# Gates and the inputs of an SSD scan, projected in one phase by block products and kept in DRAM

## The chip, the cores and the metric

One core of a Trainium2 chip runs the kernel alone. The metric is the device time of one execution in microseconds, as the median of several runs. Of the core's engines, TensorE (PE) multiplies matrices into PSUM, VectorE (DVE), ScalarE (ACT) and GpSimd (POOL) work element by element, and SyncE (SP) issues the DMAs. Each has its own queue of instructions, and semaphores tie them together.

## The reference

One layer of a hybrid encoder trunk on 1024 frames of 1024 features, in float32: a mixer of two parallel branches with a residual, a SwiGLU block with a residual, a last norm.

```python
D_MODEL = SEQ = 1024; CONV_W = 4; SSD_INNER = 2048; SSD_HEADS = 32; SSD_GROUPS = 4; SSD_STATE = 128

def hybrid_mixer(xn, w_in, ...):
    proj = xn @ w_in
    lru_x, lru_gate, z, xbc, dt_raw, gates = _split(proj, IN_WIDTHS)   # 1024, 1024, 2048, 3072, 32, 2048
    u = causal_dw_conv(lru_x, lru_conv_w, lru_conv_b)
    h = rg_lru(u, ...)
    y_a = gelu(lru_gate) * h
    xbc = silu(causal_dw_conv(xbc, ssd_conv_w, ssd_conv_b))
    xs, Bm, Cm = _split(xbc, (2048, 512, 512))
    dt = softplus(dt_raw + ssd_dt_bias)
    y = ssd_scan(xs, dt, -exp(ssd_A_log), Bm, Cm) + ssd_D[:, None] * xs
    y = y * silu(z)
    yg = y.reshape(bsz, s, 4, 512)
    yg = yg * rsqrt(mean(yg * yg, axis=-1) + EPS)
    y_b = yg.reshape(bsz, s, 2048) * ssd_norm_g
    g_a, g_b = _split(sigmoid(gates + b_gate), (1024, 1024))
    merged = g_a * (y_a @ w_branch[:1024]) + g_b * (y_b @ w_branch[1024:])
    return merged @ w_out

h = x + hybrid_mixer(rms_norm(x, norm1_g), ...)
h = h + (silu(n @ w_gate) * (n @ w_up)) @ w_ffn_out          # n = rms_norm(h, norm2_g)
return rms_norm(h, norm_f)
```

## The kernel before

Every matrix is held as two parts, a rounded one and the rest (`split`, on ACT and DVE), and a product is three matmuls: high by high, high by low, low by high. A matmul has 128 rows of weights and 512 columns, so 128 output features on all 1024 frames take 8 blocks of the sum x 2 halves x 3 = 48 matmuls (`mm_ch`). Weights come through a plan (`add`, `w_next`): a raw block is loaded into one of two buffers, split, and used in the order of the plan.

The order of the work is this. Norm 1 makes `xn_hi` and `xn_lo`, transposed, 64 KB per partition, which stay until the last gate. The LRU branch has eight tiles, each with two projections, a convolution read out of PSUM (`conv`) and a tail on ACT and DVE (`lru_tail`), whose result goes to DRAM. Then the SSD scan runs over four groups of eight chunks of 128 frames. A group needs one tile of B, one of C and four of x (`xbc`: 48 matmuls, convolution, Silu), and z of each chunk (`gate_z`: 24 matmuls). `chunk_in` forms the decay matrix of a chunk from a row of cumulated decays read from DRAM (a difference on DVE, a mask on POOL, an exp on ACT), the scores and the transposed x; `chunk_out` multiplies, carries the state on, multiplies with Silu of z, normalizes each row and stores it. Projections of the next group stand by hand between chunks 2 and 5. Two gate tiles stand behind the last chunk. Then the branch product (`wb`), where the normalized rows come back and are transposed (`add_v`); then gates and merges by turns (`gate`, `gate_b`, `merge`); the out projection and norm 2; the first FFN product in seven block products instead of eight (`unit_sums`, `opened`, `after`); the second FFN product.

The Tile framework schedules the instructions: what stands earlier in the program has priority, and within that an instruction goes where a model of the engines sees it ready. Tiles with one tag rotate through `bufs` buffers; a pool opened where another was closed lies on its memory and waits tile by tile for its last readers.

These lines carry the step that the change rewrites in the scan:

```python
nc.vector.tensor_tensor(out=ed, in0=ed, in1=bcast(acs_t[:, c, hs], P), op=ALU.subtract)      # L541
nc.scalar.activation(out=ed, in_=ed, func=AF.Exp)                                            # L545
r = rsqrt_dve(pp, ss, 1.0 / GC)                                                              # L611
nc.vector.scalar_tensor_tensor(out=yf, in0=yf, scalar=r[:, 0:1], in1=g_bc, op0=ALU.mult, op1=ALU.mult)   # L612
```

## Time and profile before

| | |
|---|---|
| time, median of 3 runs | 2077.08 us (2075.48 to 2077.55) |
| the profiled execution, its own time | 2076.53 us |
| its span, first to last instruction | 2074.8 us |
| mean granted TensorE clock | 0.993 |
| PE, DVE, ACT, POOL busy | 2014.5, 1215.4, 837.7, 520.6 us |
| matmuls (and transposes) | 9212 |
| DMA traffic | 182 MB, mean 88 GB/s |

A profile is one execution on the chip. Lines such as L132 are lines of the program, and a line can be a helper's. A matmul's own duration (about 0.39 us) is longer than its place in the queue, since matmuls overlap; so its cost is read from a stretch that is full of them. The granted clock is 1.00 at 2.4 GHz and 0.50 at 1.2 GHz. In the chain of waits each piece is what released the next one.

### The profile page before, as it was taken

How to read it: one execution, taken by the hardware profiler on the slowest of the kernel's cores; microseconds unless marked ns; L12 is line 12 of the kernel's file. 1: busy time of each engine (PE TensorE's matmuls, PEld its weight loads, DVE VectorE, ACT ScalarE, POOL GpSimd, SP SyncE). 2: the span in 40 equal slices, each digit the busy share in tenths (PEclk: the TensorE clock that was granted, in tenths of full speed). 3: DMA queues.
4: the chain of work that ended last, by engine and by line, in shares of the span. 5: the costliest groups of instructions: out<-in, count | busy, mean ns of one | idle time of the engine just before them, and what ended most of it. 6: DMA issues, size and time to landing. Idle time of an engine off the chain costs nothing.

```text
span 2074.8 us, 23723 instructions
## 1 busy us (share of the span) xinstructions
PE 2014.5 (97%) x9212; PEld 1652.6 (80%) x9212; DVE 1215.4 (59%) x1906; ACT 837.7 (40%) x1172; POOL 520.6 (25%) x364
## 2 busy tenths in 40 slices
PE   5999999999999999899999999998999999999998
PEld 4778888878788788688888888886888888888887
DVE  7677676887877877624432123567555555546445
ACT  5877653554544544531131113344323233342112
POOL 3101004525526436300101100036433433303000
PEclk9999999999999999999999999999999999999999
DMA  4221241231322322323232112521232232256212
GB/s 134 62 68 58 61 127 51 88 100 57 92 82 67 110 73 62 101 86 93 63 115 61 51 41 82 191 93 62 72 102 72 71 102 81 76 187 194 82 61 81
DMA packets 178804, 182.27 MB, mean 88 GB/s; under 512 B 9404, under 2 KB 145028, under 8 KB 178692
## 3 DMA queue, kind: packets, MB, share of 16 engines
q1 hardware_dynamic: 178692, 180.76, 28.0%
q8 instruction: 72, 1.18, 0.2%
q14 instruction: 40, 0.33, 0.1%
HBM read 148.10 MB, written 32.64 MB: 87 GB/s over the span
## 4 chain that ended last, share of the span: by engine, by line
PE 78%; DVE 11%; DMA 3%; POOL 2%; issue 2%; ACT 2%; SPq 0%; POOLq 0%; DVEq 0%; ACTq 0%
PE mm L132 35%; PE mm L810 20%; PE mm L143 13%; PE aux L143 6%; DMA ed<-acs_dram 2%; DVE rs_t L155 1%; DVE ed L541 1%; DMA w_raw<-in_w_in_dram 1%; PE aux L421 1%; PE aux L587 1%; DVE rs_r L156 1%; DVE xd L612 1%; DVE wz L81 1%; DVE rs_t L154 1%; PE turn L512 1%
## 5 line engine op out<-in xcount | busy, mean ns | idle before, releaser
L810 PE MATMUL mm<-slot,wc 128*128 128x512 f32 x1848 | 426.9, 392 | 6.3 <-DVE slot L914 5.1
L810 PEld LDWEIGHTS mm<-slot,wc 128*128 128x128 f32 x1848 | 346.9, 188 | 84.7 <-DVE slot L914 6.7
L132 PE MATMUL mm<-xn_hi,w_hi 128*128 128x512 f32 x896 | 354.1, 395 | 1.6 <-DVE xs_a L312 1.1
L132 PE MATMUL mm<-xn_hi,w_lo 128*128 128x512 f32 x896 | 353.3, 395 | 0.0
L132 PE MATMUL mm<-xn_lo,w_hi 128*128 128x512 f32 x896 | 352.2, 393 | 1.1 <-DVE xn_lo L202 1.1
L143 PE MATMUL mm<-slot,slot 128*128 128x512 f32 (+1 forms) x924 | 213.6, 387 | 0.0
L132 PEld LDWEIGHTS mm<-xn_lo,w_hi 128*128 128x128 f32 x896 | 169.2, 189 | 38.7 <-DVE xn_lo L202 1.4
L132 PEld LDWEIGHTS mm<-xn_hi,w_hi 128*128 128x128 f32 x896 | 169.2, 189 | 38.3 <-DVE xs_a L312 1.9
L143 PEld LDWEIGHTS mm<-slot,slot 128*128 128x128 f32 x924 | 171.5, 188 | 34.8
L132 PEld LDWEIGHTS mm<-xn_hi,w_lo 128*128 128x128 f32 x896 | 169.1, 189 | 37.1
L81 DVE TENSOR_TENSOR w_lo<-w_raw,w_hi 128x1024 fp32r<-128x1024 f32 x80 | 108.1, 1351 | 138.4 <-ACT w_hi L80 138.3
L143 PE MATMUL mm<-wz,xn_hi 128*128 128x512 f32 x512 | 164.0, 398 | 0.0
L80 ACT CAST w_hi<-w_raw 128x1024 fp32r<-128x1024 f32 x80 | 83.5, 1043 | 172.9 <-PE mm L132 152.1
L143 PE MATMUL aux<-slot,slot 128*128 128x512 f32 x528 | 124.4, 389 | 0.0
L143 PEld LDWEIGHTS aux<-slot,slot 128*128 128x128 f32 x528 | 99.1, 188 | 20.6
L143 PEld LDWEIGHTS mm<-wz,xn_hi 128*128 128x128 f32 x512 | 96.0, 190 | 18.9
L143 PE MATMUL mm<-wz,xn_lo 128*128 128x512 f32 x256 | 101.8, 398 | 0.0
L848 POOL TENSOR_TENSOR u_u<-u_u,e 128x512 f32<-128x512 f32 x22 | 28.8, 1310 | 248.2 <-DVE u_u L842 238.4
L81 DVE TENSOR_TENSOR wc<-s,wc 128x512 fp32r<-128x512 f32 x88 | 76.4, 908 | 23.0 <-ACT wc L80 23.0
L132 PE MATMUL mm<-v_even,w_hi 128*128 128x512 f32 x256 | 84.7, 405 | 2.2 <-ACT v_even L201 2.2
L132 PE MATMUL mm<-v_odd,w_hi 128*128 128x512 f32 x256 | 81.9, 398 | 0.0
L80 ACT CAST slot<-w_raw 128x1024 fp32r<-128x1024 f32 x34 | 35.5, 1051 | 110.2 <-PE mm L143 50.0
(273 smaller groups left out, 3298.0 us busy)
## 6 DMA issues: line engine op xcount, KB each, us to landing
w_raw<-in_w_in_dram SPq DMA_DIRECT2D x72, 512.0 KB, 3.9
ed<-acs_dram SPq DMA_DIRECT2D x32, 512.0 KB, 3.6
w_raw<-in_w_branch_dram SPq DMA_DIRECT2D x24, 512.0 KB, 3.5
w_raw<-in_w_ffn_in_dram SPq DMA_DIRECT2D x22, 512.0 KB, 4.1
raw_pair<-in_w_ffn_in_dram SPq DMA_DIRECT2D x22, 512.0 KB, 4.3
act_dram<-act SPq DMA_DIRECT2D x22, 512.0 KB, 2.6
act_raw<-act_dram SPq DMA_DIRECT2D x22, 512.0 KB, 3.5
w_raw<-in_w_ffn_out_dram SPq DMA_DIRECT2D x22, 512.0 KB, 4.7
```

The lines of the kernel that those rows point to most:

```text
L80: nc.scalar.copy(out=hi, in_=src)
L81: nc.vector.tensor_tensor(out=lo, in0=src, in1=f32(hi), op=ALU.subtract)
L132: nc.tensor.matmul(ps[:m, :], ww[:, k, :], xx(p, k, h), start=(k == 0 and i == 0), stop=(k == nk - 1 and i == 2))
L143: nc.tensor.matmul(ps, xx(p, k), ww(q, k), start=(k == 0 and i == 0), stop=(k == nk - 1 and i == 2))
L154: nc.vector.tensor_tensor(out=t, in0=r, in1=r, op=ALU.mult)
L155: nc.vector.scalar_tensor_tensor(out=t, in0=t, scalar=-0.5, in1=v, op0=ALU.mult, op1=ALU.mult)
L156: nc.vector.scalar_tensor_tensor(out=r, in0=t, scalar=1.5, in1=r, op0=ALU.add, op1=ALU.mult)
L421: nc.tensor.matmul(pg, w[:, j, :], uu[:, hs], start=(q == 0), stop=(q == 2))
L512: nc.tensor.transpose(out=pt[:, i * P:(i + 1) * P], in_=raw[:, o:o + P], identity=ident)
L541: nc.vector.tensor_tensor(out=ed, in0=ed, in1=bcast(acs_t[:, c, hs], P), op=ALU.subtract)
L810: nc.tensor.matmul(ps, w[:, p, k, :], x[q][:, k, :], start=(start and k == 0 and i == 0), stop=(k == 3 and i == 2), skip_group_check=True)
L848: nc.gpsimd.tensor_tensor(out=d["u3"], in0=d["u3"], in1=d["e5"], op=ALU.add)
```

## The change

Behind norm 1 stands a new phase. The normalized input is kept in four quarter blocks (`xq`: two halves of the features by two halves of the frames, each in two parts). While norm 1 still turns the second half of the frames, the first halves of the gates of branch a are made on the first half of the frames (`g_first`, `g_second`), and the first of the seven products is put into DRAM for later (`e1_dram`). `row_sums` forms four sums of the quarter blocks (t1 to t4). Then 20 units run, twelve for pairs of tiles of x, B and C and eight for pairs of gates (one of branch a, one of branch b): seven products of 12 matmuls each, of which a gate unit makes five here. x, B and C are convolved from SBUF (`conv_rows`), passed through Silu and stored in DRAM; gates go through a sigmoid and into DRAM. LRU follows, both halves of each projection in it. The scan loads B, C and x by tile (`rows_of`) while the group before runs, and projects z alone, for the next group in chunks 6 and 7. In a chunk the difference on DVE becomes the bias of eight exps (one per head) on ACT; the gain of the norm moves to where rows are transposed in the branch product; two chunks share one reciprocal root, and ACT does the final scaling. Buffers for z, for the output rows and for x go up. The merges load gates (`gate_in`) instead of projecting them.

```diff
+    xq = [[[quad(slot(1)) for h in range(2)] for kh in range(2)] for p in range(2)]
...
+    def g_first(m):
+        b = bank("mm")
+        hi, lo = gw[m]
+        product(b, hi[:, 0:4], lo[:, 0:4], xc["b11"], True)
+        e1 = hbuf("e1")
+        nc.scalar.copy(out=e1, in_=b)
+        nc.sync.dma_start(out=e1_dram[m], in_=e1)
+        return b
...
+    def row_sums(k):
+        ks = slice(k, k + 2)
+        f = {}
+        for kh in range(2):
+            for h in range(2):
+                f[kh, h] = ubuf(f"f{kh}{h}", [P, 2, 512])
+                (nc.vector if kh == 0 else nc.gpsimd).tensor_tensor(
+                    out=f[kh, h], in0=f32(xq[0][kh][h][:, ks]), in1=f32(xq[1][kh][h][:, ks]), op=ALU.add)
...
+        nc.vector.tensor_tensor(out=f11, in0=f12, in1=f11, op=ALU.subtract)
+        parts("t1", f11)
+        nc.gpsimd.tensor_tensor(out=f12, in0=f22, in1=f12, op=ALU.subtract)
+        nc.vector.tensor_tensor(out=f22, in0=f22, in1=f11, op=ALU.subtract)
+        parts("t2", f22)
+        nc.gpsimd.tensor_tensor(out=f21, in0=f21, in1=f22, op=ALU.subtract)
+        parts("t3", f12)
+        parts("t4", f21)
+    for m in range(3, KT):
+        gw[m] = g_parts(m)
+        gb_[m] = g_first(m)
+        g_second(m - 1, gb_[m - 1])
+        if m == 4:
+            row_sums(0)
+        elif m == 6:
+            row_sums(2)
...
+    for i in range(4):
+        kinds += [("x", 3 * i), ("x", 3 * i + 1), ("g", 2 * i), ("x", 3 * i + 2), ("g", 2 * i + 1)]
...
+    def conv_rows(x, tile_no):
+        t = ubuf("conv", [P, S])
+        tap = [par1[:, j * 24 + tile_no:j * 24 + tile_no + 1] for j in range(4)]
+        nc.scalar.activation(out=t, in_=x, func=AF.Identity, scale=tap[3], bias=par1[:, 96 + tile_no:97 + tile_no])
+        for j in (2, 1, 0):
+            d = 3 - j
+            nc.vector.scalar_tensor_tensor(out=t[:, d:], in0=x[:, :S - d], scalar=tap[j], in1=t[:, d:],
+                                           op0=ALU.mult, op1=ALU.add)
+        nc.scalar.activation(out=t, in_=t, func=AF.Silu)
+        nc.sync.dma_start(out=xbc_dram[tile_no // 2][(tile_no % 2) * P:(tile_no % 2 + 1) * P, :], in_=t)
...
+    for n, (kind, i) in enumerate(kinds):
+        uleft[n] = 7 if kind == "x" else 5
+        useq += [(n, 6), (n, 5)] + [(n, 2)] * (kind == "x") + [(n, 7), (n, 3)]
+        if n + 1 < NU and kinds[n + 1][0] == "x":
+            useq.append((n + 1, 1))
+        useq.append((n, 4))
...
-        for h in range(2):
-            nc.scalar.activation(out=t[:, half(h)], in_=ps[h], func=func,
-                                 bias=par2[:, LG + b * KT + m:LG + b * KT + m + 1])
...
-            ps = mm_ch(w_next(), xn)
-            o = pool.tile([P, S], F32, name=tag, tag=tag, bufs=bufs)
-            conv(o, ps, par1, lambda j: j * 24 + tile_no, 96 + tile_no)
-            nc.scalar.activation(out=o, in_=o, func=AF.Silu)
-            return o
+        def rows_of(tile_no, tag, bufs, pool=pp):
+            t = pool.tile([P, S], F32, name=tag, tag=tag, bufs=bufs)
+            nc.sync.dma_start(out=t, in_=xbc_dram[tile_no // 2][(tile_no % 2) * P:(tile_no % 2 + 1) * P, :])
+            return t
...
-            nc.vector.tensor_tensor(out=ed, in0=ed, in1=bcast(acs_t[:, c, hs], P), op=ALU.subtract)
...
-            nc.scalar.activation(out=ed, in_=ed, func=AF.Exp)
+            for h in range(HG):
+                nc.scalar.activation(out=ed[:, h, :], in_=ed[:, h, :], func=AF.Exp, bias=nacs_t[:, c, h0 + h:h0 + h + 1])
...
-            xd = pp.tile([P, HG, 64], F32, name="xd", tag="xd", bufs=2)
+            xd = pp.tile([P, HG, 64], F32, name="xd", tag="xd", bufs=4)
...
-            r = rsqrt_dve(pp, ss, 1.0 / GC)
-            nc.vector.scalar_tensor_tensor(out=yf, in0=yf, scalar=r[:, 0:1], in1=g_bc, op0=ALU.mult, op1=ALU.mult)
+            pend.append((c, yf))
+            if n:
+                r = rsqrt_dve(pp, ss2[0], 1.0 / GC, 2)
+                for i, (cc, y) in enumerate(pend):
+                    nc.scalar.activation(out=y, in_=y, func=AF.Copy, scale=r[:, i:i + 1])
+                    nc.sync.dma_start(out=y_dram[g][:, :, cc * P:(cc + 1) * P], in_=y.rearrange("p (a b) -> p a b", b=P))
+                pend.clear()
...
-                state = chunk_out(g, c, c_hl, parts, state, szs.pop(0), g_bc)
+                elif g + 1 < NG:
+                    if c + 2 == NC:
+                        wz_next(4)
+                    szs.append(gate_z(g + 1, c + 2 - NC))
+                state = chunk_out(g, c, c_hl, parts, state, szs.pop(0))
```

## Rows read from the trace of the kernel before

**Rows 1.** The page: each engine's busy us, share of the span, instructions.

```profile
PE 2014.5 (97%) x9212; PEld 1652.6 (80%) x9212; DVE 1215.4 (59%) x1906; ACT 837.7 (40%) x1172; POOL 520.6 (25%) x364
```

**Rows 2.** Table by stage: stretch, its length, then busy us (instructions).

```profile
core 0: us, PE busy (x) PEld busy (x) DVE busy (x) ACT busy (x) POOL busy (x), PEclk, DMA share, GB/s
0.00:46.00 46.00, 24.11 (x119) 19.14 (x120) 34.29 (x69) 24.59 (x48) 18.45 (x15) 1.00 0.47 151
457.00:604.20 147.20, 143.27 (x707) 119.01 (x706) 117.45 (x231) 73.99 (x99) 63.04 (x50) 0.99 0.27 81
751.20:875.60 124.40, 116.38 (x584) 95.42 (x584) 85.62 (x181) 57.35 (x84) 61.53 (x48) 0.95 0.24 75
1057.00:1298.00 241.00, 241.00 (x1056) 198.02 (x1055) 65.26 (x73) 57.76 (x74) 17.08 (x6) 1.00 0.25 73
1398.00:1421.00 23.00, 13.57 (x51) 9.34 (x49) 19.75 (x18) 15.83 (x22) 18.56 (x10) 0.93 0.00 1
1421.00:1825.00 404.00, 404.00 (x1765) 331.36 (x1766) 219.87 (x282) 128.32 (x229) 145.93 (x102) 1.00 0.28 86
```

**Rows 3.** Timeline of PE, last group: start us, us, instruction.

```profile
770.67 1.22 PE L587 MATMUL aux<-xdt,ed 128*128 128x64 f32 x10
...
817.91 0.78 PE L587 MATMUL aux<-xdt,ed 128*128 128x64 f32 x6
```

**Rows 4.** Table by stage, in the last group's chunks with z alone beside them.

```profile
771.70:818.70 47.00, 45.79 (x232) 38.16 (x232) 39.40 (x78) 23.58 (x35) 33.23 (x26) 0.93 0.20 63
805.00:810.00 5.00, 4.78 (x16) 3.61 (x15) 2.67 (x7) 0.15 (x1) 2.31 (x2) 0.50 0.41 125
```

**Rows 5.** Groups by line, whole span, DVE: two of FFN, one of LRU.

```profile
L81 DVE TENSOR_TENSOR wc<-s,wc 128x512 fp32r<-128x512 f32 x88 | 76.4, 908 | 23.0 <-ACT wc L80 23.0
L842 DVE TENSOR_TENSOR u_u<-mm,e_sg 128x512 f32<-128x512 f32 x22 | 15.2, 691 | 36.3 <-PE mm L810 36.3
L429 DVE SCALAR_TENSOR_TENSOR th<-gr,th 128x1024 f32<-128x1024 f32 x8 | 9.8, 1222 | 0.2
```

**Rows 6.** LRU's end: the chain of waits on PE, and DVE's timeline.

```profile
249.41 60.21 PE mm L132 x263
...
257.64 1.23 DVE L433 TENSOR_TENSOR gr<-gl,gr 128x1024 f32<-128x1024 f32 x1
```

**Rows 7.** Groups by line of ACT in the second group of the scan.

```profile
L545 ACT ACTIVATE ed<-ed 128x1024 f32<-128x1024 f32 x8 | 8.5, 1060 | 1.8 <-POOL ed L543 1.8
L465 ACT ACT_TABLE_LOAD x5 | 6.4, 1283 | 19.0 <-DVE keep L315 9.4 <-DVE b_ch L315 4.2 <-DVE xs_b L315 3.1
L80 ACT CAST w_hi<-w_raw 128x1024 fp32r<-128x1024 f32 x6 | 6.2, 1033 | 0.0
L565 ACT CAST xw<-xwf 128x512 fp32r<-128x512 f32 x7 | 4.3, 620 | 17.4 <-POOL xwf L563 17.3
L465 ACT ACTIVATE xs_b<-xs_b 128x1024 f32<-128x1024 f32 x3 | 3.2, 1061 | 3.1 <-DVE xs_b L315 3.0
L307 ACT ACTIVATE xs_b<-mm,par 128x512 f32<-128x512 f32 x4 | 3.1, 774 | 1.5 <-PE mm L132 1.5
```

**Rows 8.** Groups by line of DVE in the same stretch.

```profile
L541 DVE TENSOR_TENSOR ed<-ed,acs_t 128x1024 f32<-128x1024 f32 x8 | 12.9, 1612 | 5.2 <-DMA ed<-acs_dram 5.2
L612 DVE SCALAR_TENSOR_TENSOR xd<-xd,rs_r,g_bc 128x512 f32<-128x512 f32 x8 | 7.7, 966 | 0.3
L312 DVE SCALAR_TENSOR_TENSOR xs_b<-mm,par,xs_b 128x509 f32<-128x509 f32 x5 | 3.7, 743 | 0.1
```

**Rows 9.** The chain of waits in the last group: start us, us, what.

```profile
806.78 2.74 DMA y_dram<-xd
```

**Rows 10.** Timeline of ACT in the last group: start us, us, instruction.

```profile
791.49 0.60 ACT L532 ACTIVATE sz<-mm 128x512 f32<-128x512 f32 x1
792.11 1.28 ACT L545 ACT_TABLE_LOAD   x1
793.40 1.06 ACT L545 ACTIVATE ed<-ed 128x1024 f32<-128x1024 f32 x1
```

More of the change, by code (lines that the diff above doesn't have):

```diff
@@ L274, in params, with u_raw, product @@
             nc.vector.tensor_copy(out=dst[:, :n], in_=pt[:, :n])
+    def u_raw(name, col, stage=None):
+        t = stream.tile([P, KT, P], F32, name="w_raw", tag="w_raw", bufs=2) if stage is None else ubuf(name, [P, KT, P])
+        nc.sync.dma_start(out=t, in_=w_cols(w_in, col))
+        return t
+    xc = {"b11": [xq[p][0][0] for p in range(2)], "b21": [xq[p][1][0] for p in range(2)],
+          "b22": [xq[p][1][1] for p in range(2)]}
+    XOF = {1: "b11", 2: "b21", 3: "b22", 4: "t4", 5: "t1", 6: "t2", 7: "t3"}
+    def product(ps, whi, wlo, x, start):
+        for k in range(4):
+            for i, (w, q) in enumerate(((whi, 0), (whi, 1), (wlo, 0))):
+                nc.tensor.matmul(ps, w[:, k, :], x[q][:, k, :], start=(start and k == 0 and i == 0),
+                                 stop=(k == 3 and i == 2), skip_group_check=True)
     norm1_load(0)
@@ new lines, in g_first, with gate_out @@
+    def g_first(m):
[6 more added lines that the diff above has]
+        return b
+    def gate_out(b, m, h, src, dst=None):
+        o = hbuf("g_out") if dst is None else dst
+        nc.scalar.activation(out=o, in_=src, func=AF.Sigmoid, bias=par2[:, LG + b * KT + m:LG + b * KT + m + 1])
+        nc.sync.dma_start(out=g_dram[b][m][:, half(h)], in_=o)
@@ new lines, in g_second @@
+    def g_second(m, b):
+        hi, lo = gw.pop(m)
+        product(b, hi[:, 4:8], lo[:, 4:8], xc["b21"], False)
+        gate_out(0, m, 0, b)
+    gw = {0: g_parts(0)}
+    gb_ = {0: g_first(0)}
+    params()
+    late_rows = [norm1_rows(c) for c in range(4, 6)]
+    gw[1] = g_parts(1)
+    gb_[1] = g_first(1)
+    g_second(0, gb_[0])
+    for i, c in enumerate(range(4, 6)):
+        norm1_turn(c, late_rows[i])
+    late_rows = [norm1_rows(c) for c in range(6, 8)]
+    gw[2] = g_parts(2)
+    gb_[2] = g_first(2)
@@ new lines, in hybrid_block_kernel, with unit_prepare @@
+    HOME = {1: 1, 2: 1, 6: 6, 7: 6, 4: 6, 5: 5, 3: 5}
+    NU = len(kinds)
+    useq, uleft = [(0, 1)], {}
+    for n, (kind, i) in enumerate(kinds):
[4 more added lines that the diff above has]
+        useq.append((n, 4))
+    def unit_prepare(i):
+        if i >= len(useq):
+            return
+        n, p = useq[i]
+        if n not in sums:
+            unit_sums(n)
+        t = ubuf("wc", [P, 2, 4, P], F32R)
+        split(t[:, 0], t[:, 1], sums[n][p])
+        wready[n, p] = t
+        uleft[n] -= 1
+        if uleft[n] == 0:
+            if n + 2 < NU:
+                unit_load(n + 2)
+            elif n + 2 == NU:
+                load_next()
+                load_next()
@@ new lines, in hybrid_block_kernel @@
+    unit_load(0)
+    unit_load(1)
+    ULEAD = 3
+    for i in range(ULEAD):
+        unit_prepare(i)
+    g_second(KT - 1, gb_[KT - 1])
+    for i, (n, p) in enumerate(useq):
+        unit_prepare(i + ULEAD)
+        if HOME[p] == p:
+            banks[n, p] = bank("mm")
+        w = wready.pop((n, p))
+        product(banks[n, HOME[p]], w[:, 0], w[:, 1], xc[XOF[p]], HOME[p] == p)
+        unit_after(n, p)
+    t_stack.close()
+    u_stack.close()
+    wst_stack = ExitStack()
+    wst = wst_stack.enter_context(phase("wst", "right"))
@@ L650, in v_odd, with add_ya, then @@
             return t
+        ya = []
+        def add_ya(j):
+            def then(raw):
+                t = slot(1)
+                split(t[:, 0, :], t[:, 1, :], raw)
+                ya.append(t)
+            add(ya_dram[j * P:(j + 1) * P, :], then)
         for g in range(NG):
@@ L657, in hybrid_block_kernel @@
                     add_v(g + 1, m // 2, v_even if g % 2 else v_odd)
-        add(w_cols(w_in, OFF_G))
+                if g >= 2:
+                    add_ya((g - 2) * 4 + m // 2)
+        for m in range(KT):
+            add(w_cols(w_branch, m * P))
         for g in range(NG):
@@ L741, in hybrid_block_kernel @@
         add_wo(0, 0, wo0)
-        merge(KT - 2, gas.popleft())
-        merge(KT - 1, gas.popleft())
+        gas = deque(gate_in(0, m) for m in range(2))
+        for m in range(KT):
+            gate_b(m)
+            if m + 2 < KT:
+                gas.append(gate_in(0, m + 2))
+            merge(m, gas.popleft())
         w_drain()
@@ L760, in hybrid_block_kernel @@
     split_half(0, 0)
-    r8[1] = ctx.enter_context(phase("r8b"))
     wo1, wo2 = [], []
```

283 lines of the change are left out of this document (149 added, 134 removed).

## The prediction

> **What bounds the kernel now.** I read the page's busy shares first: TensorE (PE) is busy for 2014.5 of 2074.8 us [rows 1], so what it lacks is 60.3 us in all, and any gain must come from PE work or from those 60. The table by stage then shows where they lie [rows 2]: 21.9 us in norm 1, 3.9 to 4.1 us in each of the first three groups of the scan (one row stands for three), 8.0 us in the last group, 9.4 us at the turn from out projection to FFN. The FFN stage, which already uses the seven-product scheme that the change brings to the projections, has PE busy for all of its 404 us, and so has the stretch of gates and merges: 1056 matmuls in 241.0 us, 0.228 us each. That last number is the price of a matmul in all that follows. So the kernel is PE-bound nearly everywhere, the scan included, and the scan is so because projections of B, C and x fill PE between its chunks. Third, the one stretch where chunks run with z alone beside them, in the last group: 771.7 to 818.7 us. Four chunks pass in it (score-times-x products end at 771.9 and at 818.7 us, [rows 3]), 11.7 us per chunk, and there VectorE (DVE) is busy for 39.4 of 47 us, 84%; the granted clock is 0.93 over it, and after PE has small gaps it is 0.50, its lower level, for 5 us [rows 4]. That stretch is what the change makes of the whole scan, with a lighter DVE.
>
> **The change, part by part.** The sum is made against the profiled execution: span 2074.8 us, 2076.5 us with what lies around it, 0.6 us below the median of 2077.1.
>
> *Matmuls.* Before, 24 tiles of B, C, x and 16 of gates take 48 matmuls each: 1920. After, 12 units of B, C, x take 7 products of 12 matmuls, 1008, and 8 units of gates the same 7 products (two of them early, in norm 1), 672: 1680. 240 fewer at 0.228 us is **-54.8 us** on PE [rows 2]. z, LRU, branch and output products keep their counts. This term has one answer wherever PE is the bound.
>
> *Start.* Norm 1 keeps its chain; instead of the first halves of an LRU tile, PE gets 192 matmuls of gate column products on the first half of the rows, 43.8 us, and the LRU halves come later in full. I cost it at 0: the gap up to 46 us is set by x loads and DVE, both unchanged (bounds -3 and +4 us).
>
> *The operand sums.* The blocks t1 to t4 of the normalized input have to be formed and split. DVE has 12 passes of 1024 elements at about 1.2 us for that, some 15 us without and 20 us with a slow GpSimd (POOL) beside it, and PE has five gate columns, 27 us, as cover; DVE also splits five weights in it (7 us) and comes out of norm 1 with 34.3 of 46 us busy [rows 2]. The nearest row is the same step before FFN, 9.4 us of idle PE with a granted clock of 0.93, and that has less cover [rows 2]. I take **+5** (0 to +9).
>
> *The units.* 1488 matmuls in 339 us. For a unit of x (84 matmuls, 19.2 us) DVE has seven splits at 0.91 us, four additions at 0.69 us and six convolution passes of 1024 elements, for which the nearest is a three-operand pass of LRU at 1.22 us [rows 5]: 6.4 + 2.8 + 7.3 = 16.5 us, 86% of PE. A gate unit needs 7.3 of 13.7 us. Three of the one and two of the other give 64 of 85 us, 75%, where FFN has 220 of 404, 54% [rows 2]. PE stays the bound, but an addition that must be read out of a bank before the next product enters it can stand behind three convolution passes: **+5** (0 to +20). POOL has five passes per unit as in FFN, where it is busy for 146 of 404 us. 46 MB of new DRAM traffic (12.6 + 8.4 + 2.1 written, and read once) and 104 transfers more in SP's queue stay beside that, since FFN moves 86 GB/s with PE full [rows 2]; a store that waits for its Silu holds the next unit's weights behind it in that queue, and two units of lead cover it.
>
> *From units to LRU.* The weight pool of LRU is opened on memory that the last unit's buffers leave, so the first LRU weight waits for some of them, then for its split; I take the last unit's addition and store, **+5** (0 to +12). The block-diagonal weights of LRU lie behind 96 matmuls and hide.
>
> *Into the scan.* Before, PE runs from LRU straight into B and x products at 249.4 us while the last LRU tile's tail is finished on DVE (last product at 257.6 us, 1.2 us long) [rows 6]. After, only z of two chunks, 10.9 us, stands there. The tiles of x rows lie on LRU's buffers, so their loads follow the tail and its store, then take about 4 us, then PE can transpose. PE is through its work at about 256 us and the rows come at about 265 us: 9 us, and some 3 us for a clock that has fallen [rows 4]. **+12** (+3 to +20).
>
> *The chunks.* PE's own work per chunk is 24 matmuls of z, 5.5 us, and 3.7 us of scores, states, outputs and transposes: 9.2 us. ScalarE (ACT) is what becomes tight. A group of eight chunks now has 74.0 us of it [rows 2]. Away go the Silu of six tiles, 6.4 us, their five table loads, 6.4, twelve Identity passes at 0.774, 9.3, and six weight casts, 6.2 [rows 7]: 45.7 us left. In come the 64 exps of 128 elements in place of 8 of 1024. From 1.06 us for 1024 and 0.62 us for 512 elements a straight line gives 0.29 us for 128: 18.6 instead of 8.5 us (from 8.5, if the fixed part overlaps, to 39.7 at the price of a 512 pass). In come 8 scalings of 0.62, 5.0 us, and five table loads, because Silu of z no longer shares a load with Silu of a tile, 6.4 us. Together 67.2 us, **8.4 us per chunk**. POOL keeps its 63.0 us, 7.9 per chunk. DVE loses 36 long convolution passes at 0.743, 26.7 us, the 12.9 us of differences and the 7.7 us of final scaling [rows 8]: 117.5 us come down to 70, 8.8 per chunk at the most, and by six weight splits and half of the normalizer's small passes to less. So three engines stand at 85 to 95% of PE. From the measured stretch, DVE at 84% of the pace, I take the same share for ACT: 8.4 / 0.84 = 10.0 us per chunk. It is not 11.7, because DVE no longer has 39.4 / 4 = 9.9 us per chunk [rows 4], and because waits like the 2.74 us for the store of a chunk's output [rows 9] go with four such buffers instead of two. Bounds: 9.4 (PE alone) and 11.7 us (the stretch as it was). The scan had lost 19.9 us idle and 10 us at the lower clock (0.01 of three groups, 0.05 of the last) [rows 2]. At 10.0: 32 x 0.8 - 29.9 = **-4 us** (-24 to +50). What is queued behind: PE's in-order queue holds the products of a chunk behind z, so a late state or a late exp stops z too once three z tiles wait.
>
> *A rule against this part.* Between Silu and Exp the trace has a table load of 1.28 us which begins 0.02 us after the pass before it and is followed by the Exp at once [rows 10]. The Trainium skill (ScalarE: Activation LUTs, What ACT_TABLE_LOAD costs) puts a drain of 1380 ns on top of each load. By the rows a switch costs 1.28 us and the sum stays as below; by that rule ACT would have 2 x 1.38 us more per chunk, 11.2 us, and the sum would be some 38 us higher. The same section gives an ACTIVATE with a bias operand about 280 ns + 0.833 ns per element, less 93 ns back to back; by that, an estimate, 64 small exps would cost 18.8 us, and no run here has such an exp.
>
> *Out of the scan and after.* Gates were the filler behind the last chunk; now branch weights have to come: **+4** (0 to +8). The merge stage loses its gate products and loads gates instead: per merge 10.9 us of PE against 2.8 us of POOL and 4.1 us of DVE; 0.
>
> Sum: -54.8 + 5 + 5 + 5 + 12 - 4 + 4 = **-27.8 us**, so 2048.7 us for an execution like the profiled one and **2049 us** beside the median.
>
> **The rivals.** *The scan leaves PE.* ACT, POOL and PE hand chunks to each other in order, ACT waits in its queue for POOL, and each gap drops the clock as at 805 us [rows 4]. If the pace stays at 11.7 us, the scan's term is +50 instead of -4: -54.8 + 50 + 31 = +26, **2103 us**. It decides from a pace of 10.9 us per chunk on, where all is lost that seven products save. For it: the measured stretch. Against it: a third less DVE work and deeper buffers.
> *All is hidden.* Pace 9.4 us, handovers together 10 us instead of 31: -54.8 - 24 + 10 = -69, **2008 us**. For it: FFN shows that PE can be full in such a scheme; against it: every handover of the kernel before shows a gap.
> *The units are bound by DVE.* With convolution passes at 1.4 us beside POOL and splits late, an x unit takes 21 us and a gate unit 1 us more: +30 instead of +5, **2074 us**, no change.
> *A table switch costs more than its load.* If what surrounds a switch costs as much again as the load, 1.28 us twice per chunk, ACT stands at 11.0 us, more than PE, and can't go faster: 32 x 1.8 - 29.9 = +28 instead of -4, **2081 us** at least. Against it: the rows of such switches show no gap [rows 10]. The rule of the Trainium skill (ScalarE: Activation LUTs) named above says this.
>
> **How the numbers follow.** Forecast 0.46, all hidden 0.20, scan leaves PE 0.23, units bound by DVE 0.08, dearer switches 0.03. The range runs from 2005 to 2110: it takes in the fast case and the slow one, and leaves out handovers that all cost their upper bound and a pace above 11.9 us. A measurement of this kernel can tell about 0.2%, 4 us, from no change. Faster: the forecast but for 0.01, the fast case, half of the unit case, 0.69. Same: 0.05, from the unit case and the edges of the forecast and the slow one. Slower: 0.26, the slow case and the dearer switches for the most part.
>
> **What would show it.** Right: about 8970 matmuls instead of 9212; PE busy without a gap through 340 us of units; chunks 10.0 us apart; ACT the second busiest engine in the scan, at 80 to 90%; a gap of some 10 us ahead of the first chunk. Wrong: the granted clock below 0.9 over the scan, or chunks more than 10.9 us apart, makes it slower; gaps of several us in each x unit with DVE above 90% point to the convolutions; a first chunk right behind LRU and 9.4 us per chunk make it faster than I say.

## The result and the profile after

The changed kernel takes **2142.9 us** (median of 4 runs, 2142.5 to 2145.2) against 2076.3 us for the kernel before on the same chip (2074.9 to 2077.6): ratio 1.032, 95% interval 1.031 to 1.034. It is slower by 67 us, where I forecast 2049 us with a range of 2005 to 2110. Its profiled execution took 2142.7 us, with a span of 2140.8 us.

The page of the changed kernel: busy time of each engine, then PE and the granted clock in 40 slices of the span.

```profile
PE 2018.7 (94%) x8972; PEld 1636.9 (76%) x8972; DVE 1282.9 (60%) x1695; ACT 965.2 (45%) x1545; POOL 697.0 (33%) x472
...
PE   6899999989999998898799999998999999999998
...
PEclk9999999999999999999599999999999999999999
```

Against [rows 1] PE has 240 matmuls less, as the diff says, and is busy for longer all the same: over the scan its granted clock is 0.94 and 0.58 (below), where it was 0.95 to 0.99 before [rows 2]. The time lies in three places for the most part, which the table by stage of the changed kernel separates (columns as in [rows 2]; in order: norm 1 with the gate columns, the units, the entry into the scan, the scan while z lasts, the scan behind the last z, the first FFN product).

```profile
core 0: us, PE busy (x) PEld busy (x) DVE busy (x) ACT busy (x) POOL busy (x), PEclk, DMA share, GB/s
0.00:96.00 96.00, 64.74 (x268) 51.37 (x269) 81.05 (x94) 48.11 (x79) 54.43 (x26) 0.91 0.51 158
96.00:459.00 363.00, 345.02 (x1480) 278.53 (x1478) 266.13 (x277) 179.23 (x246) 158.16 (x97) 0.99 0.38 115
...
672.00:717.00 45.00, 44.26 (x209) 36.33 (x208) 16.36 (x18) 24.10 (x39) 8.33 (x7) 1.00 0.42 164
717.00:1004.00 287.00, 258.31 (x1322) 212.24 (x1321) 191.79 (x330) 205.21 (x423) 199.21 (x159) 0.94 0.36 116
1004.00:1075.00 71.00, 49.32 (x190) 38.38 (x188) 43.30 (x89) 43.74 (x94) 42.37 (x37) 0.58 0.29 90
...
1481.00:1886.00 405.00, 405.00 (x1743) 328.20 (x1743) 211.54 (x279) 127.37 (x228) 140.12 (x101) 1.00 0.27 84
```

- *Start.* The 268 PE instructions up to 96 us are about 58 us of work at full clock (202 products of 512 columns at 0.228 us, the other 66 as in [rows 2]). 38 us are lost, 22 us before.
- *Units.* 1480 matmuls at 0.228 us are 337 us; the stage takes 363, so 26 us are lost.
- *Scan.* From 672 to 1075 us it takes 403 us, with 952 matmuls of 512 columns. The scan before (309.6 to 876.0 us) takes 566.4 us with 1936 of them, and both have the same 764 small products. The 984 fewer are 224 us at 0.228 us, and the stage is only 163 us shorter: 61 us are lost beyond what was lost before. In 717 to 1004 us no engine is full: PE 90%, DVE 67%, ACT 71%, POOL 69%. PE has run z ahead, issues the last z at 1004 us, and from there has little but the last chunks' own products, at a clock of 0.58 on average, between its levels of 1.2 and 2.4 GHz.

Losses beyond those of the kernel before: 16 + 26 + 61 us, and by the same count of 512-column matmuls 7 us in LRU (459 to 672 us), 5 us in the branch product and the merges behind the scan and 6 us in the first FFN product (below), 121 us in all. Less the 55 us of matmuls that is the 66 us by which the spans differ.

The chunks' products of scores and x in the changed kernel, all 32 chunks in one group: durations in ns, then start of the first and of the last.

```profile
L782 PE MATMUL aux<-xdt,ed x512: 217/275/477, 714.6 to 1063.4; 128*128 128x64 f32 x171
```

Chunk 0 ends at 716.9 us and chunk 31 at 1063.8 us: 31 steps of **11.19 us**, where I had taken 10.0 and called anything above 10.9 slower.

### The profile page after: what moved, and what is told of

Same layout as the page of the kernel before. It is cut to its first block, busy times and chain, and to the rows that moved or that the text cites. A ratio compares the mean times of both kernels' runs of the same rounds, so it can differ in the third digit from the quotient of the medians.

```text
span 2140.8 us, 23980 instructions
## 1 busy us (share of the span) xinstructions
PE 2018.7 (94%) x8972; PEld 1636.9 (76%) x8972; DVE 1282.9 (60%) x1695; ACT 965.2 (45%) x1545; POOL 697.0 (33%) x472
## 4 chain that ended last, share of the span: by engine, by line
PE 48%; DVE 1%; ACT 1%; issue 0%; ACTq 0%; DVEq 0%
PE mm L308 19%; PE mm L134 13%; PE mm L145 10%; PE aux L145 6%; PE turn L705 1%; PE aux L206 0%; DVE slot L1092 0%; ACT slot L1091 0%; DVE o L1256 0%; DVE xb L1077 0%; DVE xr L1061 0%; DVE t L1081 0%; DVE wc L83 0%; DVE rs_t L163 0%; DVE xb L1083 0%
## 5 line engine op out<-in xcount | busy, mean ns | idle before, releaser
L308 PE MATMUL mm<-slot,wc 128*128 128x512 f32 x2376 | 564.5, 396 | 14.8 <-DVE wc L83 8.2
L308 PEld LDWEIGHTS mm<-slot,wc 128*128 128x128 f32 x2376 | 447.7, 189 | 124.1 <-DVE wc L83 10.6
L134 PE MATMUL mm<-slot,w_hi 128*128 128x512 f32 x768 | 243.6, 398 | 8.7 <-ACT w_hi L82 8.7
L308 PE MATMUL mm<-t,wc 128*128 128x512 f32 x960 | 228.2, 394 | 11.8 <-ACT wc L82 7.1
L145 PE MATMUL mm<-wz,slot 128*128 128x512 f32 x768 | 208.2, 418 | 17.3 <-ACT sz L725 12.9
L308 PEld LDWEIGHTS mm<-t,wc 128*128 128x128 f32 x960 | 181.7, 190 | 53.4 <-ACT wc L82 14.6
L145 PEld LDWEIGHTS mm<-wz,slot 128*128 128x128 f32 x768 | 149.0, 200 | 53.6 <-ACT sz L725 16.6
L134 PEld LDWEIGHTS mm<-slot,w_hi 128*128 128x128 f32 x768 | 145.9, 190 | 43.6 <-ACT w_hi L82 9.2
L134 PE MATMUL mm<-slot,w_lo 128*128 128x512 f32 x384 | 151.5, 396 | 0.0
L435 DVE SCALAR_TENSOR_TENSOR conv<-rows,par,conv 128x1023 f32<-128x1023 f32 (+2 forms) x72 | 111.0, 1541 | 17.3 <-ACT conv L432 17.3
```

Source lines behind the costliest of these rows:

```text
L134: nc.tensor.matmul(ps[:m, :], ww[:, k, :], xx(p, k, h), start=(k == 0 and i == 0), stop=(k == nk - 1 and i == 2))
L145: nc.tensor.matmul(ps, xx(p, k), ww(q, k), start=(k == 0 and i == 0), stop=(k == nk - 1 and i == 2))
L308: nc.tensor.matmul(ps, w[:, k, :], x[q][:, k, :], start=(start and k == 0 and i == 0), stop=(k == 3 and i == 2), skip_group_check=True)
L435: nc.vector.scalar_tensor_tensor(out=t[:, d:], in0=x[:, :S - d], scalar=tap[j], in1=t[:, d:], op0=ALU.mult, op1=ALU.add)
```

## The experiments

All edits are made to the changed kernel, whose time is 2142.9 us; every kernel was timed beside the kernel before, whose medians were 2075.2 to 2077.0. One thing limits what small differences in the scan say. The Tile framework orders each engine's queue when the program is built, so an edit upstream also reorders the scan: the changed kernel and the one with a store moved ahead of it (below) run the same 404 passes of DVE in the scan in two different orders. Four kernels with the same scan code (the changed one, and three below with edits ahead of the scan only) had paces of 11.19, 11.57, 11.63 and 11.91 us. A difference in the scan of less than about 20 us is therefore not read as the effect of an edit. The changed kernel has the lowest of the four paces, so a gain that is counted from it is not flattered.

### Which engine sets the chunks' pace

**Without the exponentials.** The eight `activation(... func=AF.Exp, bias=nacs_t...)` of a chunk taken out, `fill=0.0`.

> Leaves out the exponentials of the decay block in the scan (the eight ACT passes of a chunk and with them the two table loads; masked places are filled with 0). Everything else of the changed kernel stays. The changed kernel's scan runs at 11.19 us a chunk. Theory A (ACT's in-order queue sets the pace): a chunk loses 2.45 us of passes and up to two loads of 1.28, the pace falls to 10.0 or less and the time by 35 to 60 us, to 2085-2108. Theory B (the buffers held by the paired normalizer and its stores) and theory C (PE, with its z products): the pace stays within 0.4 us of 11.2 and the time above 2130. Theory D (a chain through all queues in which no engine is full): the pace falls by part of the 5 us, to about 10.5, time 2115-2130.

2135.2 us, pace 10.82. ACT fell from 244 to 113 us of the scan and only 8 us came back, where theory A asked for 35 to 60: ACT alone does not set the pace.

**Half of z.**

```diff
-mm_tok(zp, ..., lambda p, k: wz[k // 2][:, p, k % 2, :], KT)
+mm_tok(zp, ..., lambda p, k: wz[k // 2][:, p, k % 2, :], KT // 2)
```

> Leaves out half of the z projection's products (12 of the 24 matmuls of a chunk, 384 of 8972 in all). Theory C (PE sets the pace of the scan): 12 x 0.228 = 2.7 us less a chunk, the pace falls from 11.2 to 8.5 and the time by 70 to 88 us, to 2055-2075. Theories A, B, D (something else sets it): the pace stays at 10.8 to 11.4, the time within 15 us of 2143 and PE waits longer in the scan by what it no longer does.

2179.0 us, pace 12.19: 384 matmuls fewer and 36 us *slower*, which no theory had. The table row over its scan (columns as above):

```profile
717.00:1095.00 378.00, 270.73 (x1186) 222.31 (x1186) 225.53 (x402) 230.07 (x498) 234.27 (x194) 0.75 0.31 99
```

The clock is 0.75 where the changed kernel has 0.88 over its scan. The work taken out did not shorten the scan at all, so it was not the amount of PE's work that the chunks waited for. What PE still has to do became slower: a product of scores and x takes 421 ns (median) instead of 275. How much of the 31 us by which this scan is longer comes from that, and how much from the new order of the queues, no run separates.

**One chunk at a time.** The normalizer and the store for each chunk by itself: `if n:` becomes `if True:`, `ss2` and the root one column wide.

> Undoes the pairing alone: each chunk is normalized and stored by itself, with the four output buffers kept. Theory B (output buffers held until the second chunk of a pair is normalized): the waits of the D-term pass for the store (15.7 us in 717-1004) go, the pace falls to 10.2-10.6 and the time by 18 to 30 us, to 2113-2125. Theory E (DVE's small passes, held up beside POOL's, cost more than they show): twice as many small passes of 0.3 to 0.9 us, so the pace rises by 0.5 to 2 us and the time to 2155-2200. Theories A, C: within 6 us of 2143.

2160.1 us, pace 11.56. The wait for the store of a paired buffer (L761 below, 18.8 us) is gone and the scan got no faster; but the edit also brings more small passes, 372 that take 121 us for 180 that take 76, so it does not weigh the buffers alone. By itself the 17 us are within what reordering does.

**One exponential.** The difference back on DVE (`tensor_tensor(... bcast(acs_t[:, c, hs], P), op=ALU.subtract)`), one `Exp` over 1024 columns.

> Undoes the move of the decay difference to ACT alone: DVE subtracts the running sum over 128x1024 (about 1.2 us a chunk) and ACT takes one pass of 1024 columns in place of eight of 128. Theory A: ACT loses about 1.4 us a chunk, the pace falls to about 10.2 and the time by 20 to 30 us, to 2113-2123. Theory E (DVE beside POOL is the tight pair) : DVE gains 1.2 us a chunk, the pace rises to 11.8-12.4 and the time to 2160-2180. Theories B, C, D: within 10 us of 2143.

2148.2 us, pace 11.37, too little to read.

**A third decay buffer.** `tag="ed", bufs=2` becomes 3 (and `c_ch` 2 becomes 1, for room).

> One size changed: three buffers for the decay block in place of two (and, to make room, one buffer of C rows in place of two). In the changed kernel each decay buffer goes round in 22.57 us: its load is issued 0.31 us after the product that frees it, 5.74 to the masking, 1.19 masking, 1.25 wait, 2.69 exponentials, 4.92 wait, 1.21 multiplication, 2.95 wait, 2.32 product; two of them give 11.3 us a chunk. Theory F (this ring of two sets the pace): with three the pace falls to what PE (9.2) or POOL (8.3) want, 9.4 to 10.3, and the time by 30 to 55 us, to 2088-2113. Theory D (the ring only follows a pace set by the order of the other steps): the turn of a buffer grows to about 33 us, the pace stays at 10.8-11.5 and the time within 12 us of 2143.

2139.6 us, pace 10.99. The ring of two buffers follows the pace and doesn't set it; theory F fell.

**POOL relieved.** The addition of `yo` and the low part of `state_hl` from `nc.gpsimd` to `nc.vector`.

> Moves two of POOL's seven passes of a chunk to DVE: the addition of the state's output (1.30 us) and the low part of the state (1.28 us). Theory E (POOL's two-input passes, and DVE's small passes that stretch from 0.16 to 1.2 us beside them, set the pace): the pace falls from 11.19 to 10.0-10.5 us and the time by 20 to 35 us, to 2108-2123. Theory D (a chain through all queues in which no engine is full, ACT 86, DVE 81, PE 63, POOL 57 us of the 347 us): the pace stays within 10.8-11.6 and the time within 15 us of 2143.

2139.1 us, pace 11.07: too little to read, and not the 10.0 to 10.5 of theory E. The normalizer's small passes on DVE, of which more below, fell from 76 to 51 us in this scan, and DVE had POOL's two passes to do in their place.

So none of these, engine, ring or move, sets the pace by itself. Followed back from the last chunk's product through the changed kernel's scan, the chain of waits is 347 us long and holds ACT for 86, DVE for 81, PE for 67 and POOL for 57 us. I looked in it for passes that are longer than their data, and found the normalizer's. DVE's groups in the scan of the changed kernel, 717 to 1064 us (line, shapes, count, busy us, mean ns, idle time before them); left out are those that say nothing here:

```profile
L762 DVE TENSOR_TENSOR ed<-ed,aux 128x1024 f32<-128x1024 f32 x31 | 37.5, 1208 | 0.3 <-PE aux L740 0.3
L801 DVE TENSOR_TENSOR xd<-aux,xd 128x512 f32<-128x512 f32 x32 | 21.9, 686 | 15.8 <-POOL xd L800 9.8 <-PE aux L782 6.0
...
L761 DVE TENSOR_TENSOR xd<-turn,d_bc 128x512 f32<-128x512 f32 x30 | 20.6, 685 | 18.8 <-DMA y_dram<-xd 18.8
...
L165 DVE SCALAR_TENSOR_TENSOR rs_r<-rs_t,rs_r 128x2 f32<-128x2 f32 x45 | 18.5, 411 | 1.3
...
L164 DVE SCALAR_TENSOR_TENSOR rs_t<-rs_t,rs_v 128x2 f32<-128x2 f32 x45 | 16.0, 357 | 1.2
L163 DVE TENSOR_TENSOR rs_t<-rs_r 128x2 f32<-128x2 f32 x45 | 14.4, 320 | 1.2
L172 DVE TENSOR_SCALAR rs_i<-rs_v 128x2 int32<-128x2 int32 x15 | 12.8, 854 | 0.4
...
L170 DVE TENSOR_SCALAR rs_v<-ss 128x2 f32<-128x2 f32 x15 | 7.4, 496 | 13.6 <-ACT sz L807 13.5
L174 DVE TENSOR_SCALAR rs_r<-rs_i 128x2 int32<-128x2 int32 x15 | 6.7, 444 | 0.3
```

180 passes over two columns take 75.8 us, a third of DVE's time in the scan and twice its multiplication of the decay block. The timeline of one root shows why (start, us, engine, line; instructions between are left out):

```profile
852.64 1.28 POOL L794 TENSOR_TENSOR state_hl<-state,state_hl 128x512 fp32r<-128x512 f32 x1
852.94 1.00 DVE L163 TENSOR_TENSOR rs_t<-rs_r 128x2 f32<-128x2 f32 x1
853.88 1.30 POOL L803 TENSOR_TENSOR xd<-xd,sz 128x512 f32<-128x512 f32 x1
853.97 1.22 DVE L164 SCALAR_TENSOR_TENSOR rs_t<-rs_t,rs_v 128x2 f32<-128x2 f32 x1
...
855.13 1.05 POOL L790 TENSOR_TENSOR state<-state,dec_t 128x512 f32<-128x512 f32 x1
855.23 0.97 DVE L165 SCALAR_TENSOR_TENSOR rs_r<-rs_t,rs_r 128x2 f32<-128x2 f32 x1
856.13 1.30 POOL L759 TENSOR_TENSOR xw<-xwf,xw 128x512 fp32r<-128x512 f32 x1
856.23 1.22 DVE L163 TENSOR_TENSOR rs_t<-rs_r 128x2 f32<-128x2 f32 x1
...
857.48 0.16 DVE L164 SCALAR_TENSOR_TENSOR rs_t<-rs_t,rs_v 128x2 f32<-128x2 f32 x1
```

Each of these first four small passes (852.94 to 857.45) ends within 0.02 us of the end of the POOL pass beside it; the next one slips in behind POOL's next pass and waits for that as well. With no POOL pass beside it the same pass takes 0.16 us. Over the scan 111 of the 180 ran alone, at 0.160 us, and 69 beside POOL (an overlap of over 0.05 us), at 0.841; 61 of the 69 end within 0.03 us of the end of a POOL pass. Passes with an operand in PSUM don't wait: of L801, 20 beside POOL take 685 ns and 11 alone 686. DVE works in order, so a root of 9.6 us (848.2 to 857.8, with 2.8 us of other passes between its own) holds up the next chunk's passes.

The pairing, which the change brought in, has a share in this. The root's passes with one input (TENSOR_SCALAR) are held at two columns: 30 of them beside POOL took 813 ns, 15 alone 167. In the kernel before they have one column, and 54 of them beside POOL in its scan took 151 ns, 38 alone 143; in the changed kernel's scan with one chunk at a time they have one column again, and 63 beside POOL took 150. The row of one of them in the kernel before, second group:

```profile
L163 DVE TENSOR_SCALAR rs_i<-rs_v 128x1 int32<-128x1 int32 x8 | 1.2, 148 | 0.2
```

Half as many roots did not halve the cost: from the first chunk's product to the last, 362 small passes took 91 us before, and 180 take 76 us now.

The Trainium skill (SBUF — State Buffer, SBUF: two separate sides) states this: VectorE and GpSimd contend for one pair of SBUF ports, a VectorE operation with two SBUF inputs or in a two-port mode takes it, and whoever starts first holds it for its whole instruction. The trace agrees for passes with two inputs in SBUF, in which of them wait (not those with one in PSUM) and in how long (to the end of POOL's pass); whether the passes with one input and two columns run in a two-port mode, no row shows.

**Without the normalizer.** Squares, root, scaling and pairing out; each chunk stored as it is.

> Leaves out the normalizer of the scan (square and its sum, reciprocal root, scaling, pairing); each chunk is stored as it is. In the changed kernel's chain of waits through the scan DVE's small passes of it are 45 us and ACT's squares and scalings 18 us of 347. Theory E (the small passes beside POOL set the pace): the pace falls below 10.0 and the time by 35 to 55 us, to 2088-2108. Theory D (other chains stand right behind): as with the exponentials, a third of its share at most, the pace stays above 10.5 and the time falls by 5 to 22 us, to 2121-2138.

2105.0 us, pace 10.04: 38 us back, inside theory E's range of times (its pace, below 10.0, is just missed), almost five times what the exponentials gave. PE now holds 176 of the chain's 311 us. The scan without the normalizer:

```profile
717.00:1028.50 311.50, 287.42 (x1501) 240.62 (x1501) 162.81 (x223) 204.54 (x417) 236.21 (x193) 0.92 0.39 124
```

**The normalizer taken late.** This one keeps the computation. The root is taken once per group, and POOL, nearly idle behind the scan, scales the rows when they come back:

```diff
+nc.scalar.activation(out=sz, in_=yf, func=AF.Square, accum_out=ssg[g][:, c:c + 1])
+nc.sync.dma_start(out=y_dram[g][:, :, cs], in_=yf...)
+if c == NC - 1:
+    nc.vector.tensor_copy(out=rg[g], in_=rsqrt_dve(pp, ssg[g], 1.0 / GC, NC))
 # add_v, ahead of the transposes
+nc.gpsimd.tensor_tensor(out=rv, in0=rv, in1=bcast(rg[g], P), op=ALU.mult)
```

> Keeps the normalizer but takes it out of the chunks' way: squares stay in each chunk, the output is stored as it is, the reciprocal root is taken once per group of eight chunks (12 small passes in place of 48), and the scaling is done by POOL on the loaded tile ahead of its transposes. Theory E (the root's small DVE passes, 69 of 180 of them held beside POOL's at 0.84 us, stand in the chain of every second chunk): the pace falls to 10.0-10.4 and the time to 2102-2118. Rival (ACT's squares, or the order of stores, were what the run without a normalizer took away): the pace stays above 10.7 and the time above 2125.

2120.4 us, pace 10.36. The pace is inside theory E's range; the time is 2 us above it, with a longer way out of the scan (12.7 us from the last chunk to the branch product, 11.4 in the changed kernel). The squares stayed and the pace fell, so it is not the squares. Three things left the chunks here: most of the root (36 small passes in the scan that take 12.7 us, for 180 that took 75.8), the scalings on ACT (30 that took 20.0 us), and the wait of each store for the root. That the root is what counts is argued: 131 us taken off ACT gave 8 us, and with one chunk at a time the wait for stored buffers was gone too, without a gain; no run takes the root out by itself. The scan with the late normalizer:

```profile
717.00:1038.40 321.40, 287.03 (x1496) 237.61 (x1496) 173.58 (x261) 221.54 (x476) 241.59 (x197) 0.92 0.38 121
```

### What covers the rest

**Three x pairs back in the scan.** `kinds` loses the pairs 3, 5 and 7; their four tiles of weights are planned behind z of the group ahead, and `xs_part` (24 matmuls on two banks in each of the chunks 2 to 5, then `conv` and Silu) makes the tiles that `rows_of` would load. One buffer of C rows in place of two makes room.

> Moves work back: three of the eight x pairs (the second pair of groups 1 to 3) leave the block-product units and are projected in the scan as before, 96 matmuls a pair with their convolution, over the chunks 2 to 5 of the group ahead (one buffer of C rows in place of two). The units lose 3 x 84 matmuls, 62 us at the changed kernel's 363 us for 1476; the scan gains 288 matmuls or 66 us of PE work. Theory C (PE sets the scan's pace): the scan grows by the 66 us, the time is 2140-2155. Theories A, D, F (PE is not what the scan waits for, and waits at half clock): the scan grows by 0 to 30 us, its clock rises above 0.95, and the time is 2081-2111.

2100.1 us, 43 us back. The row over its scan:

```profile
643.00:1018.00 375.00, 349.06 (x1801) 290.55 (x1800) 251.14 (x469) 264.24 (x538) 234.86 (x195) 0.95 0.35 108
```

The units end 66 us earlier (388.5 for 454.3 us) and the scan grew by 28 us for 66 us of added PE work: 38 us of it ran where PE had waited or had a low clock. This is the change undone in part, and it shows what the projections in the scan had been worth.

**Both.**

> The late normalizer together with three x pairs projected in the scan (2100.1 us by themselves). PE then has 32 x 9.2 + 66 = 360 us of its own in the scan, which took 375 with the x pairs alone. If both remove the same idle time of PE, the scan falls to 360-368 us and the time to 2083-2095; if they were losses that add up, 2060-2075.

2076.4 us, level with the kernel before (ratio 0.9999, 0.999 to 1.001). The two gains, 43 and 22.5 us, add up to within about 1 us, which speaks for two losses and against the same idle time seen twice; the forecast for two losses, 2060 to 2075 us, was missed by 1 us, and with orders that shift a scan by 20 us so close a sum is in part luck. The scan:

```profile
643.70:997.00 353.30, 343.22 (x1799) 289.49 (x1799) 207.93 (x326) 243.31 (x506) 241.44 (x198) 0.96 0.36 115
```

**One exponential, and POOL relieved, where DVE has room.** The two edits from above, in the fastest kernel (below).

> The fastest kernel so far (2072.0 us) with the decay difference back on DVE and one exponential of 1024 columns in place of eight of 128, as in the kernel before. In the changed kernel this undoing cost 5 us. If it was DVE, kept by the normalizer's small passes, that made it dear there, DVE now has room (209 of 353 us busy) and ACT's 1.4 us a chunk come back: 2062-2070. If the difference is dear beside POOL in any case, or ACT isn't waited for, 2071-2080.

> The kernel before this one with two of POOL's passes of a chunk (2.6 us) moved to DVE as well. If POOL is the next to be waited for, another 3 to 8 us faster; if PE's own 360 us now set the scan, within 3 us; if DVE becomes the tight one again (some 270 of 350 us), slower by 2 to 8 us.

2080.2 and 2075.1 us against 2072.0. Both differences lie below the 20 us that a new order can make (the paces are 11.69 and 11.55 for 11.38), so they don't tell which form is better, and neither do the 5 us between the two. The undoing has come out slower both times that it was tried by itself, by 5 and 8 us, so there is no sign that eight small exponentials on ACT are a loss.

### Ahead of the scan

**Units without convolutions.** The three passes of `for j in (2, 1, 0)` in `conv_rows` out.

> Leaves out the 72 convolution passes of the units (three DVE passes of about 1.5 us per tile); everything else stays. Theory G (these passes, 111 us in the 363 us of the units, hold up the evacuations and weight splits that PE waits for): the units fall from 363 to 340-346 us and the time to 2120-2127. Rival (the units lose time elsewhere, at weight loads or at matmul starts): the units stay above 355 us and the time above 2135.

The units' stage fell to about 344 us and LRU starts at 439.6 instead of 463.4 us; the time is 2131.6 us, above the 2120 to 2127 of theory G, because the scan, in another order, took 12 us more. The groups of the units: DVE's convolutions and PE's products in the changed kernel,

```profile
L435 DVE SCALAR_TENSOR_TENSOR conv<-rows,par,conv 128x1023 f32<-128x1023 f32 (+2 forms) x72 | 111.0, 1541 | 17.3 <-ACT conv L432 17.3
```

```profile
L308 PE MATMUL mm<-t,wc 128*128 128x512 f32 x960 | 228.2, 394 | 11.8 <-ACT wc L82 7.1 <-DVE rows L455 4.8
```

and the same products without them:

```profile
L308 PE MATMUL mm<-t,wc 128*128 128x512 f32 x960 | 223.5, 389 | 0.0
```

The waits are gone, so theory G holds for the units: PE waits behind convolution passes of 1.54 us each.

**Row sums on DVE alone.** `nc.gpsimd` becomes `nc.vector` in `row_sums`.

> Moves the eight POOL passes of the row sums to DVE; everything else stays. In the changed kernel DVE's passes of 1.2 us take 2 to 6 us beside them, and the stage up to the first unit ends near 96 us. Theory H (POOL's two-input passes slow DVE's): DVE's passes go back to 1.2-1.5 us, and the first unit starts 2 to 8 us earlier, time 2135-2141. Rival (the stage is short of DVE time as such): DVE gains eight passes, about 10 us, and the first unit starts 2 to 10 us later, time 2145-2153.

2152.1 us, but the 193rd matmul of the block products starts at 79.9 instead of 93.8 us, and the first one on the new sums at 84.6 instead of 96.6. (The single passes on DVE that the expectation has at 2 to 6 us take 3.4 us at most in the changed kernel.) The units gave 12 of the 14 us back (PE waited 21 instead of 14 us there), the way to LRU took 4 us less, and the scan, in another order, took 14 us more. In the fastest combination, where the order of the scan stays nearly the same (pace 11.38 for 11.40), the edit shows by itself:

> The kernel before this one with the row sums on DVE alone. By itself that edit brought the first unit 14 us forward and lost 12 of them again in the units, where PE waited for DVE. With nine pairs instead of twelve in the units DVE has less to do there: 3 to 10 us faster than the kernel without it. Rival (the units' DVE work is short in every unit, not on average): within 3 us of it, or slower.

**2072.0 us** (2069.8 to 2076.0), 4 us below the kernel without it, and ratio 0.9982 (0.997 to 0.999) to the kernel before: the one version whose interval lies below the kernel before, by 0.2%. DVE's weight splits in the first 96 us, with the sums partly on POOL (first) and on DVE alone (second):

```profile
L83 DVE TENSOR_TENSOR g_lo<-w_raw,g_hi 128x1024 fp32r<-128x1024 f32 x8 | 15.5, 1944 | 0.5 <-ACT g_hi L82 0.3
```

```profile
L83 DVE TENSOR_TENSOR g_lo<-w_raw,g_hi 128x1024 fp32r<-128x1024 f32 x8 | 11.1, 1394 | 0.5 <-ACT g_hi L82 0.3
```

Eight passes more on DVE cost less than their company on POOL did.

**A lead of four.** `ULEAD = 4` in that kernel.

> The kernel before this one with the units' weights split four products ahead instead of three. If PE waits in the units for weights that are split too late (7 of the 12 us of waits that the trace shows there are for a split), 2 to 7 us faster; if it waits for banks that DVE empties late behind convolution passes, within 2 us.

2077.6 us; the units end at 389.5 instead of 386.3 us. Splitting earlier doesn't help; that it makes the units 3 us longer neither of the two expectations had, and the cause is open.

**The last LRU store on POOL.** The scan's first loads stood in SP's queue behind the store of the last LRU tile. SP's timeline in the changed kernel, then with that store issued by POOL:

```profile
673.11 19.50 SPq L657 DMA_DIRECT2D ya_dram<-gr  x2
692.71 0.38 SPq L678 DMA_DIRECT2D c_ch<-xbc_dram  x1
```

```profile
674.28 0.34 SPq L657 DMA_DIRECT2D ya_dram<-gr  x1
678.61 0.34 SPq L678 DMA_DIRECT2D c_ch<-xbc_dram  x1
684.07 9.68 SPq L678 DMA_DIRECT2D xs<-xbc_dram  x4
```

> One edit: the store of the last LRU tile is issued by POOL instead of SP. In the changed kernel that store waits in SP's queue from 673 to 692.6 us, and the scan's first loads behind it are issued from 692.7 on. Theory I (the queue sets the entry): the loads are issued as soon as their buffers come free, the first chunk's product ends at 697-706 instead of 716.9 us and the time falls by 10 to 20 us, to 2123-2133. Rival (the loads wait for LRU's buffers, which the same last DVE pass frees): the first product stays at 712-718 us and the time within 6 us of 2143.

> Both edits that moved the time down or may do so: three x pairs projected in the scan (2100.1 us by itself) and the store of the last LRU tile on POOL. If the two add up as theory I has it, 2080-2092; if the entry is set by LRU's buffers, 2096-2104.

The first load is issued 14 us earlier, but the last of the four x loads only 1.6 us (693.4 for 695.0 us), right behind the end of DVE's last LRU pass (693.36), and the first chunk ends no earlier, at 718.7 us. So the loads do wait for LRU's buffers, as the rival has it, and PE is full of z meanwhile (44.2 of 45 us). The times are 2167.5 and 2109.6 us, 24 and 9 us slower than without the edit, with paces of 11.91 and 12.52. I have no cause for that but the new order of the scan; it is open.

## Why the prediction was wrong

Forecast and measurement are 94 us apart: 49 us in the scan with its entry and its way out, 34 us ahead of it, 6 in the first FFN product and 5 in the branch product and the merges.

- **Matmuls, -54.8.** The count is right (8972). In the first FFN product, which the change doesn't touch, matmuls start 232.4 ns apart instead of 228.9 (1400 matmuls in the middle of the stage), 6 us in all, and every kernel derived from the changed one has 232.4 or 233.3. No run settles why.
- **Start and operand sums, 0 and +5: +16.** The passes that I priced at 1.2 us take about 2 us beside POOL (L387, the splits of the sums, 2022 ns in the kernel with late normalizer and x pairs, 1354 with the sums on DVE). I had reckoned with "a slow GpSimd (POOL) beside it", and let it cost 5 us.
- **Units and the way to LRU, +5 and +5: +26 and +7.** A convolution pass takes 1.54 us, not 1.22, and a weight split 0.96 on average, not 0.91 (the 79 splits of sums 1.03): DVE is busy for 266 of 363 us. In size that is the rival "units bound by DVE" nearly in full (1.4 us a pass, +30), to which I gave 0.08, although DVE has 27% to spare; taking the passes out returned 19 of the 26 us.
- **Into the scan, +12.** PE did not idle there, as I had it. It ran z of seven chunks ahead, and idled and slowed down at the end instead: 71 us behind the last z at a clock of 0.58.
- **The chunks, -4: the step that failed.** Two things in it. I named ACT as the engine that becomes tight, at 8.4 us a chunk; it had 7.6, its exponentials started 0.293 us apart as the line through two sizes had it (0.29), and taking all of them out gave 8 us. And from "DVE at 84% of the pace" I made 10.0 us, as if one engine's share set the pace. At the measured 11.19 us my sum has +34 for this term instead of -4. The pace came from a chain in which no engine is full, and the part of it whose removal gave most was one that I waved off with "half of the normalizer's small passes to less": taken out with all of the normalizer it gave 38 us, taken late 22.5. Its 180 small passes take 76 us; those with two inputs were held beside POOL in the kernel before already, while projections filled PE. With the entry and the way out, the scan lost 61 us more than before, against my +12.
- **The rival "scan leaves PE"** (2103 us, 0.23) named the direction and the point from which it decides, 10.9 us; its pace of 11.7 was close to the measured 11.19, and my sign of being wrong, a clock below 0.9 over the scan, held with 0.88. I put it second because DVE had a third less work; that relief lay in passes with operands in PSUM, one big subtraction and the final scaling, and not in the small passes or in what DVE waited for. The three losses came together, which no case of mine did: my range added them one at a time.
- **Table switches.** In the scan 48 loads of 1283 ns; the one at 851.08 us begins 0.02 us after the pass before it, and the first exponential follows 0.01 us after its end. All 48 begin within 0.02 us, 46 are followed within 0.02 us, and the other two within 0.61. The drain of 1380 ns that the Trainium skill (ScalarE: Activation LUTs, What ACT_TABLE_LOAD costs) puts on top doesn't show in any row here.

## What to carry to other kernels

Before work is moved out of a stage, ask what it covered: a projection between the steps of a scan costs PE time by the count, but it also hides the chain and holds the clock, and 38 of 66 us came free when it was put back. Price a chain by its passes' latency and by which engine runs beside each of them, not by busy shares; tiny passes on DVE that read only SBUF are dear wherever POOL is at work (0.84 us instead of 0.16 here), so collect them (here once per group instead of once per pair). When an edit's effect is small, see whether the order of the queues changed with it.

## What the runs showed of the hardware

With half of the scan's z matmuls taken away (384 of 768) the scan was longer, 378 instead of 347 us, and PE was busy for 270.7 us at a granted clock of 0.75 where more work had taken 303.6 us at 0.88. A DVE pass over two columns of SBUF took 0.16 us alone and up to 1.29 us beside a POOL pass, 61 times of 69 ending with a POOL pass, while DVE passes that read PSUM kept their 0.69 and 1.21 us beside POOL passes. With one input and one column such a pass took 0.15 us beside POOL too; with two columns, 0.81.
